# One decoder layer on one core: expert weights in units of 16 KB per partition, 11 ring slots for 22, and the last weights in plain order

## The chip, the core and the metric

One core of one Trainium2 chip runs the whole kernel. The metric is the device time of one execution in microseconds (us); lower is better. TensorE (PE) does the matrix products and, as a separate row, loads their stationary operands (PEld); VectorE (DVE) and ScalarE (ACT) do the elementwise work; SyncE (SP) issues nearly all DMAs.

## The reference

```python
# x: (256, 1024), one layer, fp32
a = hybrid_mixer(x)                        # x @ w_in (1024 x 3344), three groups of heads, @ w_out
x = layer_norm(ALPHA * x + a)
logits = x @ w_router + b_router           # 32 experts, 4 chosen for each token
gates  = softmax(top4(logits))
for e in chosen experts of a token:        # sum over its 4 experts, weighted by gates
    gu  = x @ w_gate_up[e] + b_gate_up[e]            # 1024 -> 2048
    g   = minimum(gu[:, ::2], 7); u = clip(gu[:, 1::2], -7, 7)
    act = (u + 1) * g * sigmoid(1.702 * g)
    m  += gate * (act @ w_down[e] + b_down[e])       # 1024 -> 1024
out = layer_norm(ALPHA * x + m + sigmoid(x @ w_ple_gate + b) * (p @ w_ple_proj))
```

The weights of one expert are 8 MiB (gate and up) and 4 MiB (down), fp32; the 32 experts are 384 MiB, and each is read once.

## The kernel before

**Work.** First the mixer: 13 column blocks of w_in (1 MiB each), each split into a high and a low fp32r part by ACT and DVE (`split`, L405) into one of three `whl` buffers, and multiplied by the split x; then the attention groups, w_out, the first norm and the router. Then a loop over the 32 experts (L1357). Tokens of an expert are gathered into 64 slots by one-hot matmuls (`gather`, L1015, for four experts at a time); an expert with more than 64 tokens takes a branch (`tc.If(n_of[e] > NSLOT)`) that does the rest in 32 further slots: `over_gather`, `over_up` (L1361, L1385) and, one iteration later, `over_scatter` and `over_down` (L1403). `expert_up` (L1090) makes gate and up: for each of eight k it reads one 1 MiB unit; PE shows 8 matrix instructions for a unit. `expert_evac` (L1104) copies the result out of PSUM with ACT and DVE; `expert_act` (L1109) transposes it on PE (tiles ptg, ptu) and runs `swiglu` (L1059: six DVE operations and one on ACT). `expert_down` (L1122) reads four 1 MiB units. In iteration e the order written is: first half of up(e), the sum of the pair before (`combine_pair`), second half of up(e), the branch of L1403 for e-1, down(e-1), evacuation and swiglu of e. The results of two experts are put together (`weigh`) and added to the output sum by `combine_pair`. Iterations 9 to 12 also do the per-layer embedding (`ple`).

**Weights.** SP moves everything into one ring of `RING = 22` slots of 8 KB per partition (1 MiB), named `u` in the profile. `want` (L183) puts loads into a list; `pump` (L190) issues the head of the list whenever a slot is free; `done(key)` (L200) frees a slot after its last reader. So the loads go out in the order of the list, which is the order of use, and the head waits until a slot is free. During the mixer the ring also holds its working buffers (`temp`, L205), during the experts `act`, `swi`, `acc` and `out`: activations, swiglu buffers and y, the output sum, and the weighed y. `swi` holds swiglu's g and sg, y, and also, in the same bytes as g and sg, what the branch of L1403 writes:

```python
        rm["g"], rm["sg"], rm["y"] = carve(loaded["swi"], (8, NSLOT), (8, NSLOT), (D,))
        rm["yo"], rm["CTo"], rm["Po"] = carve(loaded["swi"], (256,), (S,), (NT, 4 * NOVER))
```

**The end.** The list ends with gate and up 31, first half; down 30; gate and up 31, second half; down 31 (`w_last`, cut by columns 512, 256, 128, 128). `issue_after(mm.ins)` (L1417) holds the second half of up(31) behind down(30). Then `last_down` (tile pyl, L1453) and `last_combine` (pcbl) work by column blocks, and the second norm ends the kernel.

**Order on an engine.** The text's order is a wish: a planner in the framework places the instructions of each engine when the program is built, moves them where their data allow it, and adds the waits. A branch with its body stays one piece.

Of the kernel before, what the change touches and what calls it, by code (L numbers as in the profile page):

```python
# [21 lines left out]
P = 128  # L22
# [11 lines left out]
LEVELS = (256, 128, 64, 32, 16, 8, 4, 2)  # L34
RING = 22
NWARM = 30
# [6 lines left out]
NRUN = NE  # L43
# [70 lines left out]
def lay_out(inp):  # L114
# [14 lines left out]
    for g in range(4):  # L129
# [19 lines left out]
        "w_last": np.stack([*cols(w_last, 0, 512).reshape(P, 2, 2048).transpose(1, 0, 2), cols(w_last, 512, 256),  # L149
                            halves(w_last, 768)]),  # L150
        "b_down": a["b_down"],
# [7 lines left out]
def kernel(ctx, tc, x, xT_in, pT_in, w_in, w_out, diff_lambda, params, bgu_in, w_gate_up,  # L159
# [9 lines left out]

    free = list(range(RING))  # L170
    where = {}
    serial = [0]

    def slot_tile(dtype=F32, pick=0):
# [8 lines left out]
    def want(key, fn, dtype=F32):  # L183
        pending.append((key, fn, dtype))

    def aside(fn):

        pending.append((None, fn, None))

    def pump():  # L190
        while pending and (free or pending[0][0] is None):
            key, fn, dtype = pending.pop(0)
            if key is None:
                fn()
                continue
            t, s = slot_tile(dtype)
            where[key] = s
            loaded[key] = fn(t)

    def done(key):  # L200
        loaded.pop(key)
        free.append(where.pop(key))
        pump()

    def temp(key, dtype=F32, pick=-1):  # L205
        t, s = slot_tile(dtype, pick)
        where[key] = s
        loaded[key] = t
        return t

    def retake(old, key, dtype=F32):
        loaded.pop(old)
        free.append(where.pop(old))
        return temp(key, dtype)

# [55 lines left out]

    xT = temp("xT").rearrange("p (k t) -> p k t", k=NK)
    def load_first_cols(u):
# [18 lines left out]

    room = {3: "act", 5: "swi", 12: "acc", 24: "out"}
    n_want = RING
    for e in range(NRUN + 1):
        units = []
        if e < NRUN:
            units += [(("gu", e, k), load_flat(w_gate_up[0, e, k * P:(k + 1) * P, :])) for k in range(NK)]
        if e >= 1:
            for i in range(4):  # L300
                if e < NRUN:
                    fn = load_blocks(w_down[e - 1, i], 2)
                else:
                    fn = load_halves(w_last[i]) if i == 3 else load_blocks(w_last[i], 4 if i < 2 else NK)
                units.append((("dn", e - 1, i), fn))
        if e == NRUN - 1:
            units = units[:4] + units[8:] + units[4:8]
        if e == BIAS_AT:
            units.insert(0, ("bd", load_bd))
        if e == LN2_AT:  # L310
            units.append(("ln2", load_ln2))
        if e in PLE_AT:
            i = PLE_AT.index(e)
            if i == 0:
                units += [("x1T", lambda u: u), ("plt", lambda u: load_pT(u))]
            units.append((("ple", i), load_blocks(w_ple_gate[i], NK)))
        for key, fn in units:
            n_want -= 1
            if -n_want in room:
                key_ = room[-n_want]  # L320
                want(key_, lambda u: u, F32R if key_ == 'out' else F32)
            want(key, fn)
            if key[0] == "ple":
                aside(lambda i=key[1]: load_proj(i))
# [10 lines left out]

    xh = temp("xh", F32R).rearrange("p (k t) -> p k t", k=NK)
    xl = temp("xl", F32R).rearrange("p (k t) -> p k t", k=NK)
    whl = [temp(("w", i), F32R).rearrange("p (a n) -> p a n", a=2) for i in range(3)]
    ct = temp("ct")
    t1u, t2u, t3u, t4u, t5u, t6u, t7u = (temp(f"t{i}") for i in range(1, 8))  # L340
    A0, A1, qs, kk = carve(t1u, (4, S), (4, P), (S,), (S,))
# [63 lines left out]
    def split(half):  # L405

        w = whl[nsplit[0] % 3]
# [161 lines left out]
    def mixed(key, old, units):  # L569

        u = retake(old, key, F32R).rearrange("p (i a k t) -> p i a k t", i=2, a=2, k=2)
        for n, i in enumerate(units):
            mix[i] = u[:, n, 0], u[:, n, 1]
# [298 lines left out]
    for n, i in enumerate(WORDER):  # L872
# [14 lines left out]
        if n == 1:  # L887
            done("m0")
    for i in range(3):
        if i not in ((nsplit[0] - 1) % 3, (nsplit[0] - 2) % 3):  # L890
            done(("w", i))
# [22 lines left out]
    normalise(1, mv1)  # L914
    for i in range(3):
        if i in ((nsplit[0] - 1) % 3, (nsplit[0] - 2) % 3):
            done(("w", i))
# [172 lines left out]
    def expert_up(e, pgu=None, ks=range(NK)):  # L1090
# [31 lines left out]
    def expert_down(e, act, y):  # L1122
        py = ps_s("py")
        for f in range(8):
            blk, j = f // 2, f % 2
            w = loaded["dn", e, f // 2]
            for nb in range(2):
                mm = nc.tensor.matmul(py[nb * 64:(nb + 1) * 64, :], act[:, j * 4 + blk, :],  # L1128
                                      w[:, f % 2, nb * 512:(nb + 1) * 512], start=f == 0, stop=f == 7)
# [5 lines left out]
        return mm  # L1135

# [69 lines left out]
    def gu_part(e):  # L1206
        return lambda k, b: loaded["gu", e, k][:, b * 512:(b + 1) * 512]

    def dn_part(e):
        if e == NRUN - 1:  # L1210
            return lambda f, q: loaded["dn", e, q if q > 1 else f // 4][:, f if q > 1 else f % 4,
                                                                       *([] if q > 1 else [slice(q * 256, (q + 1) * 256)])]
        return lambda f, q: loaded["dn", e, f // 2][:, f % 2, q * 256:(q + 1) * 256]

# [13 lines left out]
    def general():  # L1228

        n_max = load_count(cnt[0:1, NE:NE + 1])  # L1230
        with tc.If(n_max > NSLOT + NOVER):
# [9 lines left out]
            with tc.For_i(0, NRUN, 1) as ie:  # L1241
# [3 lines left out]
                with tc.If(n > NSLOT + NOVER):  # L1245
                    with tc.For_i(0, (n - (NSLOT + 1)) // NOVER, 1):
                        def up(k, b):
                            w = wst[b % 2]
                            nc.gpsimd.dma_start(w, w_gate_up[0, bass.ds(ie, 1), k * P:(k + 1) * P,
                                                           b * 512:(b + 1) * 512].squeeze(0))  # L1250
                            return w

                        def down(f, q):
                            w = wst[q % 2][:, :256]
                            nc.gpsimd.dma_start(w, w_down[bass.ds(ie, 1), f // 2, :,
                                                        (f % 2) * 1024 + q * 256:(f % 2) * 1024 + (q + 1) * 256].squeeze(0))
                            return w
# [99 lines left out]
    for e in range(NRUN + 1):  # L1357
# [51 lines left out]
        if e >= 1:  # L1409
# [12 lines left out]
        if e == NRUN - 1:  # L1422
            tc.keep_in_program_order(nc.scalar.preload_act_table_set("natural_log_exp_and_others"))
        if e >= 1 and f % 2 == 1:
# [20 lines left out]
    def last_down(c0, n):  # L1445
        h = n // 2
        py = ps_z("pyl")
        for c in range(8):
            blk, j = c // 2, c % 2
            w = loaded["dn", f, c // 4 if n == 512 else c0 // 256]  # L1450
            w = w[:, c % 4] if n == 512 else w[:, c] if n == 256 else w[:, c, c0 % 256 // P]
            for hf in range(2):
# [50 lines left out]
```

## Time and profile before

| | |
|---|---|
| median of 3 runs | 1114.71 us (1114.48 to 1115.21) |
| the profiled execution | 1113.15 us, of it 1111.5 us from first to last instruction |
| PE busy | 1041.3 us (94%); PEld 519.0 us (47%) |
| DVE, ACT, GpSimd busy | 406.2, 194.6, 7.6 us |
| DMA | 433.65 MB, mean 390 GB/s |
| TensorE clock granted, mean | 0.983 of 2.4 GHz |

Stages in the profiled execution: mixer and router to about 151 us, experts from there, the last expert's down from 1087.85 us, the end at 1111.5 us. In the profile an L number is a line of the kernel; "x32" counts instructions; the bracket at the end of a line gives the idle time of that engine before it and what ended it. A stretch of PE rows in which each begins before the one above has ended is a PE without gaps.

### The profile page before, as it was taken

The page shows a single profiled execution, that of the slowest core. Times are in us where ns is not written, and L with a number is a line of the kernel's source. Part 1 is how long each engine was busy: PE and PEld are TensorE (multiplying, and loading weights), DVE is VectorE, ACT ScalarE, POOL GpSimd, SP SyncE. Part 2 cuts the span into 40 slices and gives each one's busy share as a digit, 9 for nine tenths or more (in the row PEclk, how much of TensorE's full clock was granted, in tenths as well). Part 3 has the DMA queues.
Part 4 walks back from the last instruction along what each step waited for, and adds up shares of the span by engine and source line. Part 5 has one row for each costly group of instructions (what it writes and reads, how often), then busy time and mean ns, then how long its engine had stood idle before and what let it go on. Part 6 is the DMA issues. An engine that isn't in the chain of part 4 may idle for free. (4 is left out here: it accounts for less than half of the span.)

```text
span 1111.5 us, 13836 instructions
## 1 busy us (share of the span) xinstructions
PE 1041.3 (94%) x5330; PEld 519.0 (47%) x5330; DVE 406.2 (37%) x865; ACT 194.6 (18%) x377; POOL 7.6 (1%) x19
## 2 busy tenths in 40 slices
PE   9999999999999999999999999979999999999995
PEld 7888854333433355554543334323433443334333
DVE  4977552333333323232333223313232223323235
ACT  4447541101110111100111111101110110101011
POOL 1000000000000000000000000000000000000000
PEclk9999999999999998999999999989999999999998
DMA  9956879999999999999999999999999999999981
GB/s 346 365 217 229 310 301 387 421 419 420 421 419 421 419 419 420 418 421 418 413 419 420 420 420 420 420 419 419 420 420 420 421 420 420 420 420 419 421 372 73
DMA packets 62414, 433.65 MB, mean 390 GB/s; under 512 B 6957, under 2 KB 7469, under 8 KB 10705
## 3 DMA queue, kind: packets, MB, share of 16 engines
q1 hardware_dynamic: 62114, 431.36, 94.5%
q8 instruction: 90, 1.47, 0.5%
q0 software_dynamic: 176, 0.53, 0.1%
q14 instruction: 34, 0.28, 0.1%
HBM read 430.81 MB, written 1.06 MB: 389 GB/s over the span
## 5 line engine op out<-in xcount | busy, mean ns | idle before, releaser
L1098 PE MATMUL pgu<-u,xe 128*64 128x512 f32 x2048 | 480.0, 596 | 6.9 <-PEq L1385 0.5
L1098 PEld LDWEIGHTS pgu<-u,xe 128*64 128x64 f32 x2048 | 162.2, 137 | 282.7 <-issue 272.2
L1128 PE MATMUL py<-u,u 128*64 128x512 f32 x992 | 227.6, 607 | 35.6 <-DVEq L1403 14.7
L1128 PEld LDWEIGHTS py<-u,u 128*64 128x64 f32 x992 | 83.4, 140 | 171.8 <-issue 123.8
L1107 DVE COPY u<-pgu 128x512 f32<-128x512 f32 x32 | 22.1, 692 | 207.2 <-PE pgu L1098 207.2
L1106 ACT COPY u<-pgu 128x512 f32<-128x512 f32 x32 | 18.7, 585 | 419.9 <-PE pgu L1098 419.9
L1062 DVE TENSOR_TENSOR u<-ptg,bgu 128x512 f32<-128x512 f32 x32 | 22.1, 690 | 182.5 <-PE ptg L1116 176.4
L1133 ACT COPY u<-py 64x512 f32<-64x512 f32 x31 | 17.9, 578 | 268.8 <-PE py L1128 268.8
L1088 DVE TENSOR_TENSOR u<-u,pcb 128x512 f32<-128x512 f32 x60 | 37.5, 683 | 52.9 <-PE pcb L1087 50.0
L412 DVE TENSOR_TENSOR u<-u,u 128x1024 fp32r<-128x1024 f32 x32 | 39.0, 1223 | 15.7 <-ACT u L411 14.2
L972 DVE TENSOR_SCALAR Pr<-ci,opos 128x32 fp32r<-128x32 f32 x64 | 13.5, 237 | 85.5 <-PEq L1361 83.5
L411 ACT CAST u<-u 128x1024 fp32r<-128x1024 f32 x32 | 33.4, 1048 | 27.0 <-PE pzt L423 9.7
L1293 PE MATMUL pleg<-u,u 128*128 128x256 f32 x128 | 32.2, 407 | 2.4 <-ACT u L979 2.1
L422 PE MATMUL pzt<-u,u 128*128 128x256 f32 x128 | 32.8, 291 | 0.3 <-ACT u L411 0.3
L1087 PE MATMUL pcb<-u,PT 128*128 128x512 f32 x120 | 32.5, 411 | 0.3
L423 PE MATMUL pzt<-u,u 128*128 128x256 f32 x128 | 32.3, 288 | 0.0
L1029 PE MATMUL pgx<-Pm,xnh 128*128 128x256 f32 (+1 forms) x128 | 31.0, 285 | 0.0
L1116 PEld LDWEIGHTS ptg<-ci,u 128*128 128x128 f32 x128 | 17.8, 207 | 26.5 <-issue 25.2
L1029 PE MATMUL pgx<-Pm,xnl 128*128 128x256 f32 (+1 forms) x128 | 30.2, 279 | 0.0
L1087 PEld LDWEIGHTS pcb<-u,PT 128*128 128x128 f32 x120 | 21.4, 189 | 17.3 <-issue 13.3
L1293 PEld LDWEIGHTS pleg<-u,u 128*128 128x128 f32 x128 | 25.7, 206 | 7.2 <-ACT u L979 2.3
L1029 PEld LDWEIGHTS pgx<-Pm,xnh 128*128 128x128 f32 x128 | 24.1, 188 | 6.5 <-issue 4.9
(289 smaller groups left out, 964.0 us busy)
## 6 DMA issues: line engine op xcount, KB each, us to landing
u<-in_w_gate_up_dram SPq DMA_DIRECT2D x256, 1024.0 KB, 18.3
u<-in_w_down_dram SPq DMA_DIRECT2D x124, 1024.0 KB, 19.8
u<-in_w_in_dram SPq DMA_DIRECT2D x11, 1024.0 KB, 16.6
u<-in_w_out_dram SPq DMA_DIRECT2D x4, 1024.0 KB, 7.5
u<-in_w_ple_gate_dram SPq DMA_DIRECT2D x4, 1024.0 KB, 17.8
u<-in_w_last_dram SPq DMA_DIRECT2D x3, 1024.0 KB, 19.7
u<-in_xT_dram SPq DMA_DIRECT2D x4, 256.0 KB, 5.8
u<-in_w_in_dram SPq DMA_DIRECT2D x4, 256.0 KB, 5.6
```

Source lines behind the costliest of these rows:

```text
L411: nc.scalar.copy(wh, half)
L412: nc.vector.tensor_tensor(wl, half, wh.bitcast(F32), op=ALU.subtract)
L422: nc.tensor.matmul(pz[:, j, :], wh[:, k, :], xh[:, k, :], start=k == 0, stop=False)
L423: nc.tensor.matmul(pz[:, j, :], wh[:, k, :], xl[:, k, :], start=False, stop=False)
L1029: nc.tensor.matmul(pg[:, j, :n], v[:, t, ch], hot, start=t + i == 0, stop=t + i == NT)
L1062: nc.vector.tensor_tensor(g, pg, bg, op=ALU.add)
L1087: nc.tensor.matmul(pcb, PT[:, t * P:(t + 1) * P], v[:, sl], start=i == 0, stop=i == 1)
L1088: nc.vector.tensor_tensor(yacc[:, t, sl], yacc[:, t, sl], pcb, op=ALU.add)
L1098: nc.tensor.matmul(pgu[b][hf * 64:(hf + 1) * 64, :], xe[:, k, c0:c0 + NSLOT], w[:, b * 1024 + hf * 512:b * 1024 + (hf + 1) * 512], start=k ...
L1107: nc.vector.tensor_copy(gs[:, 1, :], pgu[1])
L1128: mm = nc.tensor.matmul(py[nb * 64:(nb + 1) * 64, :], act[:, j * 4 + blk, :], w[:, f % 2, nb * 512:(nb + 1) * 512], start=f == 0, stop=f == 7)
L1293: nc.tensor.matmul(pg[:, j, :], w[:, k, sl], x1T[:, k, :], start=k == 0, stop=k == NK - 1)
```

## The change

The weights of gate and up, and of down, are laid out in DRAM so that 16 KB per partition are contiguous: two 1 MiB units become one 2 MiB DMA. The ring has 11 slots of 16 KB per partition. A slot can be given out in two halves of 8 KB, to two things of the same type; a load of one half takes a free half if there is one, and else opens a slot; a 2 MiB load needs a whole slot. The mixer's buffers share slots in pairs, `whl` has four buffers for three, and `m1` takes the place of `xl` for that of `t6`. `act` is asked for ahead of the first expert's weights. The loads of the last weights stand in plain order (gate and up 31, down 30, down 31), `issue_after` is gone, and in iteration 31 evacuation and swiglu of 31 are written ahead of the branch of L1403 and of down(30).

```diff
-RING = 22
+RING = 11
...
-        "w_gate_up": a["w_gate_up"], "w_down": np.stack([by_rows(w, 2) for w in a["w_down"][0]]),
+        "w_gate_up": np.stack([by_rows(w, 2) for w in a["w_gate_up"][0]]),
+        "w_down": np.stack([by_rows(w, 4) for w in a["w_down"][0]]),
...
-        t = ring.tile([P, 2048], dtype, name=f"u{serial[0]}", tag=f"slot{s}")
-        return t, s
+        t = ring.tile([P, 4096], dtype, name=f"u{serial[0]}", tag=f"slot{s}")
+        halves_of[s] = [t, dtype, {0, 1}]
+        return s
+
+    def take(key, s, which):
+        t, _, rest = halves_of[s]
+        rest.difference_update(which)
+        where[key] = s, which
+        return t[:, 2048 * min(which):2048 * (max(which) + 1)]
+
+    def half_of(dtype):
+        return next((s for s, (_, d, rest) in halves_of.items() if len(rest) == 1 and d == dtype), None)
+
+    def give(key):
+        s, which = where.pop(key)
+        rest = halves_of[s][2]
+        rest.update(which)
+        if len(rest) == 2:
+            halves_of.pop(s)
+            free.append(s)
...
     def pump():
-        while pending and (free or pending[0][0] is None):
-            key, fn, dtype = pending.pop(0)
+        while pending:
+            key, fn, dtype, size = pending[0]
+            s = half_of(dtype) if size == 1 else None
+            if key is not None and s is None and not free:
+                return
+            pending.pop(0)
...
+    want("act", lambda u: u)
+    room = {4: "swi", 12: "acc", 24: "out"}
...
-            units += [(("gu", e, k), load_flat(w_gate_up[0, e, k * P:(k + 1) * P, :])) for k in range(NK)]
-        if e >= 1:
...
-        if e == NRUN - 1:
-            units = units[:4] + units[8:] + units[4:8]
+            units += [(("gu", e, j), load_flat(w_gate_up[e, j]), 2) for j in range(4)]
+        if 1 <= e < NRUN:
+            units += [(("dn", e - 1, j), load_blocks(w_down[e - 1, j], 4), 2) for j in range(2)]
+        if e == NRUN:
+            units += [(("dn", e - 1, 0), load_blocks(w_last[:, :4096], 8), 2),
+                      (("dn", e - 1, 2), load_blocks(w_last[:, 4096:6144], 8), 1),
+                      (("dn", e - 1, 3), load_halves(w_last[:, 6144:]), 1)]
...
-    whl = [temp(("w", i), F32R).rearrange("p (a n) -> p a n", a=2) for i in range(3)]
+    whl = [u.rearrange("p (a n) -> p a n", a=2) for n in (0, 2) for u in temps(("w", n), ("w", n + 1), dtype=F32R)]
+    t1u, t2u = temps("t1", "t2")
+    t3u, t5u = temps("t3", "t5")
+    t4u, t6u = temps("t4", "t6")
+    ct, t7u = temps("ct", "t7")
...
-    done("xl")
...
-    mixed("m1", "t6", (1, 2))
+    mixed("m1", "xl", (1, 2))
+    done("t6")
...
         for k in ks:
-            w = loaded["gu", e, k]
+            w = loaded["gu", e, k // 2][:, k % 2 * 2048:(k % 2 + 1) * 2048]
...
-            done(("gu", e, k))
+            if k % 2:
+                done(("gu", e, k // 2))
...
-            w = loaded["dn", e, f // 2]
+            w = loaded["dn", e, f // 4]
...
-            if f % 2:
-                done(("dn", e, f // 2))
+            if f % 4 == 3:
+                done(("dn", e, f // 4))
...
-        if e < NRUN - 1:
+        if e < NRUN:
             expert_up(e, gs_of[e], range(2 if e == 1 else NK // 2, NK))
+        if e == NRUN - 1:
+            expert_evac(gs_of.pop(e))
+            act_of[e] = expert_act(e)
+            tc.keep_in_program_order(nc.scalar.preload_act_table_set("natural_log_exp_and_others"))
...
-            mm = expert_down(f, act_of.pop(f), y)
-        if e == NRUN - 1:
-            with tc.issue_after(mm.ins):
-                expert_up(e, gs_of[e], range(NK // 2, NK))
-        if 0 < e < NRUN:
+            expert_down(f, act_of.pop(f), y)
+        if 0 < e < NRUN - 1:
             expert_evac(gs_of.pop(e))
             act_of[e] = expert_act(e)
```

## Rows read from the trace of the kernel before

**Rows 1.** The page: DMA busy share in tenths, 40 slices of the span.
```profile
DMA  9956879999999999999999999999999999999981
```

**Rows 2.** Windows: length, busy us of each engine (instructions), clock, DMA share, GB/s.
```profile
200.00:1060.00 860.00, 812.70 (x3786) 354.32 (x3784) 260.43 (x515) 100.01 (x176) 0.00 (x0) 0.98 1.01 420
...
0.00:150.00 150.00, 145.59 (x1067) 125.47 (x1068) 105.79 (x269) 80.92 (x175) 5.79 (x18) 1.00 0.78 298
```

**Rows 3.** Waits of PE from 200 to 1075 us: total, times, longest.
```profile
PE py L1128 <- DVEq L1403: 14.7, 16, 1.3
...
PE py L1128 <- DMA u<-in_w_last_dram: 1.6, 1, 1.6
...
PE py L1128 <- DMA u<-in_w_gate_up_dram: 0.9, 1, 0.9
```

**Rows 4.** The last load of down 23, by tile, 847 to 849 us.
```profile
L239 SPq DMA_DIRECT2D u<-in_w_down_dram x1: 328/328/328, 848.1 to 848.1; - x1
...
DMA to landing us min/median/max: 19.8/19.8/19.8
```

**Rows 5.** PE's timeline, start and length: down 23.
```profile
863.97 7.09 PE L1128 MATMUL py<-u,u 128*64 128x512 f32 x32 [0.89 <-DVEq L1403]
```

**Rows 6.** DMA packets and queue, 10.8 to 13.8 and 600 to 700 us.
```profile
DMA packets 517, 1.26 MB, mean 420 GB/s; under 512 B 60, under 2 KB 234, under 8 KB 505
...
q1 hardware_dynamic: 517, 1.26, 105.5%
...
DMA packets 5758, 42.02 MB, mean 420 GB/s; under 512 B 638, under 2 KB 638, under 8 KB 638
...
q1 hardware_dynamic: 5746, 41.85, 100.7%
```

**Rows 7.** Issue to landing of gate-and-up loads, 500 to 545 and 770 to 1045.
```profile
DMA to landing us min/median/max: 9.7/12.3/16.6
...
DMA to landing us min/median/max: 19.5/19.8/20.9
```

**Rows 8.** SP's timeline, 30 to 170 us: the first experts' loads.
```profile
60.00 69.92 SPq L252 DMA_DIRECT2D u<-in_w_gate_up_dram  x16
```

**Rows 9.** PE's timeline at the first expert.
```profile
151.31 6.23 PE L1098 MATMUL pgu<-u,xe 128*64 128x512 f32 x28 [0.30 <-PEq L1361]
```

**Rows 10.** Waits of PE from 14 to 150 us, the mixer: first and last of four.
```profile
PE pzn L440 <- DVE u L412: 0.8, 1, 0.8
...
PE pzt L422 <- ACT u L411: 0.3, 1, 0.3
```

**Rows 11.** PE's timeline, the end: start, length, idle before.
```profile
1065.19 2.14 PE L1087 MATMUL pcb<-u,PT 128*128 128x512 f32 x8
1068.91 7.09 PE L1128 MATMUL py<-u,u 128*64 128x512 f32 x32 [1.58 <-DMA u<-in_w_last_dram]
1075.80 7.07 PE L1098 MATMUL pgu<-u,xe 128*64 128x512 f32 x32
...
1084.11 0.52 PE L1116 MATMUL ptu<-ci,u 128*128 128x128 f32 x3
1087.85 7.11 PE L1453 MATMUL pyl<-u,u 128*64 128x256 f32 x64 [3.22 <-DVEq L1403]
```

**Rows 12.** DVE's timeline, the end: last swiglu operation of expert 31.
```profile
1087.11 0.69 DVE L1068 TENSOR_TENSOR u<-u,u 128x512 f32<-128x512 f32 x1
```

**Rows 13.** Windows ahead of, in and behind the start of pyl.
```profile
1082.90:1087.80 4.90, 1.39 (x8) 1.00 (x8) 4.04 (x7) 1.75 (x2) 0.00 (x0) 1.00 0.52 212
1088.00:1091.30 3.30, 3.30 (x18) 1.79 (x18) 0.00 (x0) 0.00 (x0) 0.00 (x0) 0.50 0.09 31
```

**Rows 14.** SP's timeline: the first three loads of down 31.
```profile
1062.31 5.29 SPq L239 DMA_DIRECT2D u<-in_w_last_dram  x3
```

**Rows 15.** All engines' timeline, 964.5 to 968.5: an ordinary expert.
```profile
966.63 0.69 DVE L1107 COPY u<-pgu 128x512 f32<-128x512 f32 x1 [7.12 <-PE pgu L1098]
...
967.48 1.51 PE L1128 MATMUL py<-u,u 128*64 128x512 f32 x6 [0.89 <-DVEq L1403]
```

More of the change, by code (lines that the diff above doesn't have):

```diff
@@ L147, in lay_out @@
         "diff_lambda": a["diff_lambda"], "params": r, "bgu": bgu.reshape(P, 512),
-        "w_gate_up": a["w_gate_up"], "w_down": np.stack([by_rows(w, 2) for w in a["w_down"][0]]),
-        "w_last": np.stack([*cols(w_last, 0, 512).reshape(P, 2, 2048).transpose(1, 0, 2), cols(w_last, 512, 256),
-                            halves(w_last, 768)]),
+        "w_gate_up": np.stack([by_rows(w, 2) for w in a["w_gate_up"][0]]),
+        "w_down": np.stack([by_rows(w, 4) for w in a["w_down"][0]]),
+        "w_last": np.concatenate([cols(w_last, 0, 512), cols(w_last, 512, 256), halves(w_last, 768)], axis=1),
         "b_down": a["b_down"],
@@ L195, in pump, with temps, retake @@
                 continue
-            t, s = slot_tile(dtype)
-            where[key] = s
-            loaded[key] = fn(t)
+            if s is None:
+                s = open_slot(dtype)
+            loaded[key] = fn(take(key, s, (0, 1) if size == 2 else (min(halves_of[s][2]),)))
     def done(key):
         loaded.pop(key)
-        free.append(where.pop(key))
+        give(key)
         pump()
[L205 to L214, printed above, removed]
+    def temps(*keys, dtype=F32):
+        s = open_slot(dtype, -1)
+        for n, key in enumerate(keys):
+            loaded[key] = take(key, s, (n,))
+        return [loaded[key] for key in keys]
+    def retake(old, key):
+        loaded[key] = loaded.pop(old)
+        where[key] = where.pop(old)
+        return loaded[key]
     def carve(t, *shapes):
@@ L270 @@
     mp = mixer.enter_context(tc.tile_pool(name="mp", bufs=1))
-    xT = temp("xT").rearrange("p (k t) -> p k t", k=NK)
+    xT = temps("xT")[0].rearrange("p (k t) -> p k t", k=NK)
     def load_first_cols(u):
@@ L291 @@
     aside(lambda: load_third())
-    room = {3: "act", 5: "swi", 12: "acc", 24: "out"}
-    n_want = RING
+    want("act", lambda u: u)
+    room = {4: "swi", 12: "acc", 24: "out"}
+    n_want = 2 * RING - 2
     for e in range(NRUN + 1):
@@ L297 @@
         if e < NRUN:
-            units += [(("gu", e, k), load_flat(w_gate_up[0, e, k * P:(k + 1) * P, :])) for k in range(NK)]
-        if e >= 1:
[L300 to L305, printed above, removed]
-        if e == NRUN - 1:
-            units = units[:4] + units[8:] + units[4:8]
+            units += [(("gu", e, j), load_flat(w_gate_up[e, j]), 2) for j in range(4)]
[5 more added lines that the diff above has]
+                      (("dn", e - 1, 3), load_halves(w_last[:, 6144:]), 1)]
         if e == BIAS_AT:
-            units.insert(0, ("bd", load_bd))
+            units.insert(0, ("bd", load_bd, 1))
         if e == LN2_AT:
-            units.append(("ln2", load_ln2))
+            units.append(("ln2", load_ln2, 1))
         if e in PLE_AT:
@@ L314 @@
             if i == 0:
[L315 to L322, printed above, removed]
+                units += [("x1T", lambda u: u, 1), ("plt", lambda u: load_pT(u), 1)]
+            units.append((("ple", i), load_blocks(w_ple_gate[i], NK), 1))
+        for key, fn, size in units:
+            n_want -= size
+            for at in [a for a in room if a <= -n_want]:
+                key_ = room.pop(at)
+                want(key_, lambda u: u, *((F32R, 2) if key_ == "out" else (F32, 1)))
+            want(key, fn, F32, size)
             if key[0] == "ple":
@@ L334 @@
     nc.vector.memset(onec, 1.0)
-    xh = temp("xh", F32R).rearrange("p (k t) -> p k t", k=NK)
-    xl = temp("xl", F32R).rearrange("p (k t) -> p k t", k=NK)
-    whl = [temp(("w", i), F32R).rearrange("p (a n) -> p a n", a=2) for i in range(3)]
-    ct = temp("ct")
-    t1u, t2u, t3u, t4u, t5u, t6u, t7u = (temp(f"t{i}") for i in range(1, 8))
+    xh, xl = (u.rearrange("p (k t) -> p k t", k=NK) for u in temps("xh", "xl", dtype=F32R))
+    whl = [u.rearrange("p (a n) -> p a n", a=2) for n in (0, 2) for u in temps(("w", n), ("w", n + 1), dtype=F32R)]
[3 more added lines that the diff above has]
+    ct, t7u = temps("ct", "t7")
     A0, A1, qs, kk = carve(t1u, (4, S), (4, P), (S,), (S,))
@@ L405, in split @@
     def split(half):
-        w = whl[nsplit[0] % 3]
+        w = whl[nsplit[0] % 4]
         nsplit[0] += 1
@@ L569, in mixed @@
     def mixed(key, old, units):
-        u = retake(old, key, F32R).rearrange("p (i a k t) -> p i a k t", i=2, a=2, k=2)
+        u = retake(old, key).rearrange("p (i a k t) -> p i a k t", i=2, a=2, k=2)
         for n, i in enumerate(units):
@@ L888 @@
             done("m0")
-    for i in range(3):
-        if i not in ((nsplit[0] - 1) % 3, (nsplit[0] - 2) % 3):
+    for i in range(4):
+        if i not in ((nsplit[0] - 1) % 4, (nsplit[0] - 2) % 4):
             done(("w", i))
@@ L914 @@
     normalise(1, mv1)
-    for i in range(3):
-        if i in ((nsplit[0] - 1) % 3, (nsplit[0] - 2) % 3):
+    for i in range(4):
+        if i in ((nsplit[0] - 1) % 4, (nsplit[0] - 2) % 4):
             done(("w", i))
@@ L1125, in expert_down @@
             blk, j = f // 2, f % 2
-            w = loaded["dn", e, f // 2]
+            w = loaded["dn", e, f // 4]
             for nb in range(2):
-                mm = nc.tensor.matmul(py[nb * 64:(nb + 1) * 64, :], act[:, j * 4 + blk, :],
-                                      w[:, f % 2, nb * 512:(nb + 1) * 512], start=f == 0, stop=f == 7)
-            if f % 2:
-                done(("dn", e, f // 2))
+                nc.tensor.matmul(py[nb * 64:(nb + 1) * 64, :], act[:, j * 4 + blk, :],
+                                 w[:, f % 4, nb * 512:(nb + 1) * 512], start=f == 0, stop=f == 7)
+            if f % 4 == 3:
+                done(("dn", e, f // 4))
         r = (e % 2) * 64
@@ L1206, in gu_part @@
     def gu_part(e):
-        return lambda k, b: loaded["gu", e, k][:, b * 512:(b + 1) * 512]
+        return lambda k, b: loaded["gu", e, k // 2][:, k % 2 * 2048 + b * 512:k % 2 * 2048 + (b + 1) * 512]
     def dn_part(e):
         if e == NRUN - 1:
-            return lambda f, q: loaded["dn", e, q if q > 1 else f // 4][:, f if q > 1 else f % 4,
-                                                                       *([] if q > 1 else [slice(q * 256, (q + 1) * 256)])]
-        return lambda f, q: loaded["dn", e, f // 2][:, f % 2, q * 256:(q + 1) * 256]
+            return lambda f, q: (loaded["dn", e, q][:, f] if q > 1 else
+                                 loaded["dn", e, 0][:, f, q * 256:(q + 1) * 256])
+        return lambda f, q: loaded["dn", e, f // 4][:, f % 4, q * 256:(q + 1) * 256]
     def over_pos(e):
@@ L1449, in last_down @@
             blk, j = c // 2, c % 2
-            w = loaded["dn", f, c // 4 if n == 512 else c0 // 256]
-            w = w[:, c % 4] if n == 512 else w[:, c] if n == 256 else w[:, c, c0 % 256 // P]
+            w = loaded["dn", f, c0 // 256][:, c]
+            w = w[:, c0 % 256 // P] if n == P else w
             for hf in range(2):
```

20 lines of the change are left out of this document (9 added, 11 removed).

## The prediction

> **What bounds the kernel now.** The first thing to look at is the DMA strip [rows 1]: from the eighth slice on every digit is a 9, and the window over the expert stage gives a DMA share of 1.01 at 420 GB/s [rows 2]. Taken alone, this says that the weights' stream sets the time. The same window has PE busy for 812.7 of 860 us, so the shares do not decide it. A wait decides it: if the stream set the time, PE would again and again stand idle until a load lands. PE's waits in the expert stage name a DMA twice, 1.6 and 0.9 us, and what else is named is the branch of L1403 [rows 3]; the 1.6 us names weights that the instruction behind the wait does not read, and I count it as the branch too.
>
> The next question is by how much the stream is ahead, and this can be worked out for any load from its issue, its time to landing and its first reader. The narrowest place that I found is down 23: its fourth and last unit goes out at 848.1 us and needs 19.8 us, so it lands at 867.9 us [rows 4]; PE starts down 23 at 863.97 us and runs through in 7.09 us [rows 5], so the fourth quarter is wanted at 863.97 + 0.75 x 7.09 = 869.3 us. That is 1.4 us to spare with both resources full. So PE bounds the expert stage and the stream follows close behind. A faster stream alone gives nothing; one that falls back by more than 1.4 us costs what lies beyond. The mixer is PE's too: 145.6 of 150 us busy [rows 2].
>
> **The 2 MiB loads.** How much faster they move is bounded from two stretches with different packets [rows 6]. Between 10.8 and 13.8 us, 517 packets less 60 small ones, 457, carry 1.26 MB, 2757 bytes each, and take 1.055 x 16 engines x 3.0 us = 50.6 us, 110.8 ns each. Between 600 and 700 us, 5758 less 638, 5120 packets of 8 KB, take 1.007 x 16 x 100 = 1611 us, 314.7 ns each. A line through both has 0.0375 ns a byte and 7.4 ns a packet. A row of 16 KB as one packet would take 622 ns where two take 629: 1.2% less. The other end is zero, if a row still goes as two packets. I take 1.2%, since the line fits both stretches; the time of the kernel gets 0 from it, because PE is the bound.
>
> The Trainium skill, "DMA: Bandwidth & Descriptors", section Bandwidth, measures 425 GB/s for 16 MB against 341 GB/s for 1 MB in one transfer and so speaks for larger loads. By its 425 GB/s the stream would gain as much as by the line (425 against the trace's 420 is also 1.2%).
>
> **The shallower ring.** Before, act, swi, acc, out leave 18 of 22 MiB for weights, 17 once ln2 is in. After, act, swi, acc and ln2 are halves of two slots and out is one: 8 slots, 16 MiB. In experts 9 to 12, x1T, plt and ple hold two more slots wholly or by half: 12 to 14 MiB where there were 15 or 16. What the missing 2 to 4 MiB are worth is read from the time to landing [rows 7]. From 770 us on it is 19.8 us at the median and never under 19.5, eight loads of 2.5 us in flight; there a smaller ring still keeps several 2 MiB loads in flight. From 500 to 545 us it is 9.7 to 16.6 us, four to six in flight, and with 2 to 4 fewer the stream can run dry. Bounds for what it loses there: 0, and two 2 MiB loads (9.9 us). Against the upper one speaks that PE is slow there because of the embedding and frees slots late in both kernels; I take 2 us. From 545 to 868 us the faster packets win back 323 x 1.2% = 3.9 us. At down 23 the stream is then 1.9 us earlier. But its third and fourth units now land together, wanted when the third begins, 863.97 + 0.5 x 7.09 = 867.5 us, against 867.9 - 1.9 = 866.0: 1.5 us to spare, no stall. Without the faster packets it would be 867.9 + 2 - 867.5 = 2.4 us of stall.
>
> **The mixer.** With slots in pairs, the first load of expert 0 needs a slot that is wholly free, so it goes out later than at the 60 us of before (when t1 and t2 are both done), the last of expert 1 when the w_out splits are through. The first reader starts at 151.3 us [rows 8, 9]: hidden; there are 91 us of cover from the old issue on. The fourth `whl` buffer can remove waits for a split, and m1's new place a wait for gog and rgg; PE's waits in this stretch are 0.8, 0.7, 0.5 and 0.3 us [rows 10]. So it is worth between 0 and -2.3 us, or a little worse if the planner orders it differently (I bound that by the same 2.3). I take 0. Half as many issues on SP (328 ns each [rows 4]) are nothing: SP issues ahead, and PE does not wait for it.
>
> **The end.** Here the change touches the path. Before [rows 11, 12, 13]: combine_pair ends at 1067.33; 1.58 us at the branch; down(30) 7.09; the second half of up(31) 7.07 to 1082.87; then the evacuation, the transposes (1082.79 to 1084.63) and swiglu, whose last operation ends at 1087.80; pyl starts at 1087.85. PE does 1.39 us of work in these 4.9 us, and when pyl starts, the granted clock is 0.50, the 1.2 GHz level, for some 3.3 us. That is 1.7 us of pyl's 7.11 lost.
>
> After, the second half of up(31) comes first, then evacuation and swiglu, then down(30). Swiglu's 4.9 us from evacuation to the last operation then run beside down(30)'s 7.09 on PE, with 2 us of cover. Sum from 1067.33: 7.07 + 1.84 + 7.09 + 1.58 for the branch = 17.6, pyl at 1084.9 instead of 1087.85: -2.9 us. If PE stays occupied, the fall of the clock is avoided too: between 0 and -1.7 us; I take -1.0, since one short wait remains. The last loads are in time: down 31 now goes out behind down 30, its first two units went out at about 1062.3 and 1065 us before [rows 14] and need some 20 us, so 1085 us, less the 1.9 us gained at 868 and a further 200 x 1.2% = 2.4.
>
> Sum: 0 (stream) + 0 (mixer) - 2.9 - 1.0 = -3.9 us. The profiled execution took 1113.15 us, 1.65 more than its span and 1.56 under the median of the runs; the difference is applied to the median: 1114.71 - 3.9 = 1110.8 us.
>
> **Rivals.**
> *PE stands behind the branch.* The branch of L1403 writes yo, CTo and Po into the bytes of g and sg, so for expert 30 it must now follow swiglu(31). down(30) stands behind it in the text, and PE has waited for DVE at just this place, 0.89 us [rows 15]. If it stays there, PE idles through swiglu: 1067.33 + 7.07 + 4.9 + 0.89 + 7.09 + 1.58 = 1088.9, which is 1.1 us later than before: 1115.8 us. Against it: the evacuation at L1107, which the text puts behind down, runs ahead of it [rows 15], so the planner does move work across this branch, and down(30) needs nothing of it.
>
> *The stream comes late.* This is the case on the slower side. Place: down 23 at 864 to 868 us. If the stretch from 430 to 545 us costs the stream two 2 MiB loads, 9.9 us, of which 3.9 come back, it is 6.0 + 0.4 = 6.4 us late: 1110.8 + 6.4 = 1117.2 us. Each us beyond the 1.5 to spare counts; over 6.1 us of stall the kernel is slower than before by more than can be told from no change.
>
> *The stream is the bound after all.* Then 1.2% of 860 us come off: 1114.7 - 10.3 = 1104.4 us. For it speaks the share of 1.01; against it the 1.4 us to spare even at the narrowest place. The Trainium skill, "Perfetto Trace Analysis", section Identifying the Most-Contended Engine, calls the matmul row's busy share a poor measure and wants the weight loads' share; here that is 354 of 860 us [rows 2], and by this rule the DMA would be the most contended and this case right. The landing times disagree.
>
> **How the numbers follow.** Overlap at the end and no stall 0.52 (1107.8 to 1113.5), behind the branch 0.25 (1113.5 to 1117.5), stream late 0.15 (1113 to 1120), stream as the bound 0.08 (1103 to 1107). The predicted time is that of the first; the range that leaves out no more than two in ten is 1106 to 1117.5. 0.2% is 2.2 us, about what a measurement of this kernel can tell from no change. Faster: 0.46 of the first and the last, 0.54; the same: 0.06 + 0.19 + 0.05 = 0.30; slower: 0.06 + 0.10 = 0.16.
>
> **What would show it.** The loads of gate and up: half as many, of 2 MiB, and a window over 600 to 700 us at about 425 GB/s (420: no faster packets). PE's waits of the expert stage still name hardly a DMA, and the last load of down 23 lands ahead of PE's reading of it. At the end, pyl starts 3 us sooner behind combine_pair, swiglu(31) lies beside py on PE, and the window behind pyl's start has the clock at 1.00. A stretch of py or pgu that ends on a DMA, at expert 23 or in 430 to 560 us, would make it wrong upwards; an idle PE beside swiglu(31) would show the first rival; a new order in the mixer that moves the first expert by more than 2 us would be outside the sum.

## The result

The changed kernel takes 1108.49 us at the median of four runs (1107.60 to 1109.14), the kernel before 1114.96 us beside it: ratio 0.994, interval 0.9927 to 0.9953. Run once more in a later comparison it took 1108.97 against 1114.28 us, ratio 0.997, interval 0.9951 to 0.999. So it is 0.3 to 0.6% faster. Of the ten later runs four took 1112.64 to 1114.59 us, at a mean granted clock of 0.979 or 0.980 where the others had 0.983 to 0.985; and one run of before_odd, told below, took 1823.55 us at a clock of 0.554 and is left out of its median and ratio. The profiled execution took 1109.14 us with a span of 1107.4 us, 4.1 us less than the span before.

The page of the changed kernel, DMA share and rate in 40 slices of 27.7 us, against [rows 1]:

```profile
DMA  9835699999999999999999999999999999999991
GB/s 346 325 151 178 274 377 428 426 426 428 426 425 427 426 423 415 425 424 394 403 428 426 426 426 426 427 425 426 426 427 424 428 427 425 427 427 427 424 383 61
```

DMA packets and queue of the changed kernel from 600 to 700 us, which answer to [rows 6]:

```profile
DMA packets 2921, 42.60 MB, mean 426 GB/s; under 512 B 320, under 2 KB 320, under 8 KB 320
## 3 DMA queue, kind: packets, MB, share of 16 engines
q1 hardware_dynamic: 2910, 42.44, 100.0%
```

A row of 16 KB does go as one packet (42.6 MB in 2921 packets, of which 320 are small: 16.4 KB in each of the 2601 others), and the stream runs at 426 GB/s where it had 420. From 166 us to the last two slices it is full, except in the two slices from 498 to 554 us (394 and 403 GB/s) and, by less, in the one from 415 to 443 us (415 GB/s).

PE's waits from 200 to 1075 us at the branch of over_down (L1430, before L1403) and for weights, to be set beside [rows 3]:

```profile
PE py L1152 <- DVEq L1430: 13.3, 15, 0.9
...
PE py L1152 <- DMA u<-in_w_down_dram: 2.5, 2, 1.3
...
PE pgu L1121 <- DMA u<-in_w_gate_up_dram: 1.0, 1, 1.0
```

PE's timeline at the end (start, length, idle before it), against [rows 11]; first the changed kernel, then two lines of the kernel before:

```profile
1053.64 7.09 PE L1121 MATMUL pgu<-u,xe 128*64 128x512 f32 x32
...
1071.44 0.52 PE L1140 MATMUL ptu<-ci,u 128*128 128x128 f32 x3
1075.28 9.68 PE L1152 MATMUL py<-u,u 128*64 128x512 f32 x32 [3.31 <-DVEq L1430]
1084.77 3.19 PE L1475 MATMUL pyl<-u,u 128*64 128x256 f32 x26
...
1095.97 1.49 PE L1484 MATMUL pcbl<-u,CT 128*128 128x128 f32 x8
```

```profile
1058.17 7.09 PE L1098 MATMUL pgu<-u,xe 128*64 128x512 f32 x32
...
1100.03 1.49 PE L1462 MATMUL pcbl<-u,CT 128*128 128x128 f32 x8
```

Three windows of the changed kernel, with the columns of [rows 13]:

```profile
1072.00:1075.20 3.20, 0.00 (x0) 0.00 (x0) 2.98 (x6) 1.82 (x2) 0.00 (x0) 0.77 0.79 329
1075.30:1080.50 5.20, 5.20 (x14) 1.70 (x16) 0.00 (x0) 0.00 (x0) 0.00 (x0) 0.50 0.56 231
1080.50:1084.70 4.20, 4.20 (x22) 1.55 (x20) 0.00 (x0) 0.00 (x0) 0.00 (x0) 0.99 0.23 94
```

The end is not what was forecast: PE stands for 3.31 us at the branch of over_down (L1430) while VectorE runs swiglu of expert 31, and its clock is at 0.50, the 1.2 GHz level, for the next 5.2 us. From the first matmul of up(31) to the end of the last pcbl the changed kernel takes 1095.97 + 1.49 - 1053.64 = 43.82 us. Before, it is 1100.03 + 1.49 - 1058.17 = 43.35 us. So the end lost 0.5 us, and the whole gain was there when expert 31 began, 4.53 us earlier than before.

**Where it comes from.** The first expert begins at 151.30 us as before [rows 9], and by the starts of up and down PE gains in two kinds of steps. Three large ones (0.85 us between experts 9 and 10, 1.69 us in expert 16, 1.59 us between 29 and 30) lie where the clock of the kernel before was at 0.50 for longer than that of the changed kernel; 0.65 us are lost between 19 and 20, where it was the other way round. Such stretches differ between executions of one kernel: at 872 to 879 us the changed kernel's was 3.4 us long here and 6.8 us in after_again.

The others are steps of 0.80 or 0.81 us, at experts 4, 6, 8, 18, 26 and 28 (PE loses steps of 0.84 and 0.82 us at 22 and 23). What differs there is the order of PE's instructions. An up has 32 matmuls, and they come in pairs: hf = 0 and hf = 1 write the two 64-row halves of one PSUM tile. The second branch over over_up (L1408, before L1385) stands somewhere in the second half of up, where the planner put it. Behind an odd number of matmuls it cuts a pair. In the program before, 25 experts have a cut pair (22 by this branch, 3 by that of over_down), in the changed one 20: at 4, 6, 8, 18, 24, 26 and 28 the branch stood behind 17 or 27 matmuls and now stands behind 24, where the last 2 MiB unit begins.

What a cut pair costs is seen in the second half of up, PE's timeline: in the changed kernel expert 27 (cut) and expert 28 (whole), then expert 28 of the kernel before (cut). A matmul here counts as two:

```profile
956.20 3.65 PE L1121 MATMUL pgu<-u,xe 128*64 128x512 f32 x14
959.99 4.48 PE L1121 MATMUL pgu<-u,xe 128*64 128x512 f32 x18 [0.15 <-PEq L1408]
...
981.14 3.65 PE L1121 MATMUL pgu<-u,xe 128*64 128x512 f32 x16
984.95 3.65 PE L1121 MATMUL pgu<-u,xe 128*64 128x512 f32 x16 [0.16 <-PEq L1408]
```

```profile
983.26 5.36 PE L1098 MATMUL pgu<-u,xe 128*64 128x512 f32 x22
988.78 2.76 PE L1098 MATMUL pgu<-u,xe 128*64 128x512 f32 x10
```

Seven matmuls take the 3.65 us of eight, and the nine behind the branch 4.48 us: from its start to its end the cut half takes 8.27 us, the whole one 7.46 us, 0.81 us less, and the same half of the kernel before 8.28 us. The two matmuls of a pair run side by side; where the branch cuts a pair, one matmul on either side of it is left alone and takes the time of a pair. Five cut pairs fewer are 4.05 us. Up to expert 31 the clock was at 0.50 for 20.5 us in place of 27.3, worth up to 3.4 us. The waits for loads took part of this back, all at one place, the second half of up 24 and down 23:

```profile
856.31 3.65 PE L1121 MATMUL pgu<-u,xe 128*64 128x512 f32 x16 [0.97 <-DMA u<-in_w_gate_up_dram]
861.31 3.65 PE L1152 MATMUL py<-u,u 128*64 128x512 f32 x16 [1.34 <-DMA u<-in_w_down_dram]
866.09 3.65 PE L1152 MATMUL py<-u,u 128*64 128x512 f32 x16 [1.12 <-DMA u<-in_w_down_dram]
```

They are 3.4 us; the first two stand where the branches cost PE 0.16 and 0.89 us elsewhere, so 2.4 us are new. The sum, 4.05 + 3.4 - 2.4 = 5.0 us, is near the 4.53 us read. In these two executions the clock is nearly as large a term as the pairs; what belongs to the change, the runs below decide.

### The profile page after: what moved, and what is told of

Same layout as the page of the kernel before. It is cut to its first block, busy times and chain, and to the rows that moved or that the text cites. A ratio compares the mean times of both kernels' runs of the same rounds, so it can differ in the third digit from the quotient of the medians.

```text
span 1107.4 us, 13426 instructions
## 1 busy us (share of the span) xinstructions
PE 1034.3 (93%) x5330; PEld 513.7 (46%) x5330; DVE 405.8 (37%) x865; ACT 194.8 (18%) x377; POOL 7.6 (1%) x19
## 5 line engine op out<-in xcount | busy, mean ns | idle before, releaser
L1121 PEld LDWEIGHTS pgu<-u,xe 128*64 128x64 f32 x2048 | 159.6, 137 | 282.2 <-issue 277.8
L1087 ACT ACTIVATE u<-u 128x512 f32<-128x512 f32 x32 | 19.9, 623 | 40.7 <-DVE u L1086 40.6
```

## The experiments

Three theories were open, with the letters of the expectations: PE is the only bound and its cut pairs made the gain (B), the faster stream made it (C), or it takes both, because PE and the stream are two bounds that lie close together (A). The experiments put the branch where it was wanted.

**The branch fixed.** `expert_up` writes the branch itself, behind `at` matmuls of the second half; for the experts from 2 on nothing else changes but that a unit is given back only behind the branch, which reads it too:

```diff
-    def expert_up(e, pgu=None, ks=range(NK)):
+    def expert_up(e, pgu=None, ks=range(NK), at=0, branch=None):
...
+                    with tc.issue_after(behind) if behind else nullcontext():
+                        mm = nc.tensor.matmul(pgu[b][hf * 64:(hf + 1) * 64, :], xe[:, k, c0:c0 + NSLOT], ...)
+                    n += 1
+                    if n == at:
+                        with tc.issue_after(mm.ins):
+                            branch()
+                        behind = nc.cur_bb.bb.instructions[-1]
...
+            expert_up(e, gs_of[e], range(2 if e == 1 else NK // 2, NK), 8 if e > 1 else 0, over)
+        if e == BIAS_AT:
+            output_bias()
```

With 8 the branch stands between whole pairs, behind 24 of 32 ("even"), with 7 inside one ("odd"). The output bias of expert 3 had to go behind the branch, since its tile shares a buffer with what the branch reads.

Of after_even was expected:

> The changed kernel with the branch in the second half of up fixed between whole pairs (24 of an expert's 32 pgu matmuls ahead of it) for experts 2 to 31. In the changed kernel it stands inside a pair for 18 experts, and a pair that is cut costs about 0.81 us (four matmuls one after the other, 0.43 us each, where whole pairs run two at a time). Theory A (PE and the stream of weights are both bounds, close together): PE has about 15 us less work, but the stream ran full at 426 to 428 GB/s from 166 us on except for about 4 us at 498 to 554 us, so no more than 2 to 5 us comes out: 1104 to 1107 us, and PE now waits for loads. Theory B (PE alone is the bound): 1093 to 1095 us. Theory C (the branch's place costs nothing, the gain came from the faster stream alone): 1108 to 1109 us.

Of after_odd was expected:

> The same, but with the branch fixed inside a pair (23 of 32 matmuls ahead of it) for all 30 experts, 11 or 12 cut pairs more than the changed kernel has. Theories A and B: PE is the bound here, 9 us more (11 times 0.81): 1116 to 1119 us. Theory C: 1108 to 1109 us.

Of before_even was expected:

> The kernel before (loads of 8 KB rows, 22 slots) with its branch fixed between whole pairs for experts 2 to 30; it has 22 cut pairs there. Theory A: its stream was full at 418 to 421 GB/s from 195 us to the end, so that 18 us less work on PE gives at most 0 to 2 us: 1113 to 1115 us, and PE waits for loads from expert 23 on. Theory B: 1095 to 1098 us. Theory C: 1114 to 1115 us, for another reason, and PE's time in the second half of up does not change.

Of before_odd was expected:

> The kernel before with the branch fixed inside a pair for experts 2 to 30, 7 cut pairs more than it has. Theories A and B: 5 to 6 us more, 1119 to 1121 us. Theory C: 1114 to 1115 us.

| run | loads | cut pairs | median us | ratio to before, interval |
|---|---|---|---|---|
| before | 1 MiB | 25 | 1114.52 | |
| before_even | 1 MiB | 0 | 1114.26 | 0.9998 (0.9988 to 1.0007) |
| before_odd | 1 MiB | all 29 of 2 to 30 | 1124.56 | 1.0077 (1.0052 to 1.0101) |
| after_even | 2 MiB | 1 | 1104.75 | 0.9913 (0.9897 to 0.993) |
| after_odd | 2 MiB | all 30 of 2 to 31, and one more | 1119.86 | 1.0052 (1.0035 to 1.0069) |

Theory A holds: without any cut pair the kernel before is no faster at all, and the changed one gains nearly 4 us more, where B wanted 1093 to 1095 us of it and C no change. Where the time that PE saves in before_even goes is seen in PE's timeline, down 21 of before and of before_even, then down 23 of before_even (before: [rows 5]):

```profile
813.20 3.23 PE L1128 MATMUL py<-u,u 128*64 128x512 f32 x14 [0.90 <-DVEq L1403]
```

```profile
803.59 5.73 PE L1139 MATMUL py<-u,u 128*64 128x512 f32 x24 [0.89 <-DVEq L1417]
809.87 1.94 PE L1139 MATMUL py<-u,u 128*64 128x512 f32 x8 [0.54 <-DMA u<-in_w_down_dram]
...
863.89 1.94 PE L1139 MATMUL py<-u,u 128*64 128x512 f32 x8 [0.90 <-DVEq L1417]
866.05 1.94 PE L1139 MATMUL py<-u,u 128*64 128x512 f32 x8 [0.23 <-DMA u<-in_w_down_dram]
868.50 1.94 PE L1139 MATMUL py<-u,u 128*64 128x512 f32 x8 [0.51 <-DMA u<-in_w_down_dram]
870.97 1.94 PE L1139 MATMUL py<-u,u 128*64 128x512 f32 x8 [0.54 <-DMA u<-in_w_down_dram]
```

PE is 9.6 us ahead at down 21 and level with before at down 23, where it waits for unit after unit. In after_even the same happens at 426 GB/s: it is 8.2 us ahead of the changed kernel at down 21 and 2.7 at down 23.

after_odd is 0.9 us and before_odd some 4 us over what was expected, though before_odd has only four cut pairs more than before (29 against 25, where the expectation counted seven), some 3.2 us. Most of the rest is the clock: up to PE's last work it was at 0.50 for 44 us of before_odd's profiled execution, in the kernel before for 31. Of the 44 us 3.4 lie at expert 3, behind the output bias that now follows the branch. PE's timeline of after_even there, where down takes 8.79 us for 7.09 (8.74 in after_odd, 8.78 in before_odd):

```profile
238.15 3.69 PE L1356 MATMUL pbd<-u,GT 32*128 32x512 f32 x8 [0.78 <-DVE GT L1351]
242.73 8.79 PE L1163 MATMUL py<-u,u 128*64 128x512 f32 x32 [0.89 <-DVEq L1444]
```

PE's waits in after_even, 200 to 1075 us (the changed kernel's: 2.5 and 1.0):

```profile
PE py L1163 <- DMA u<-in_w_down_dram: 5.4, 4, 1.6
PE pgu L1123 <- DMA u<-in_w_gate_up_dram: 5.1, 6, 1.2
```

**The size of a load alone, with whole pairs.** after_even, with each 2 MiB load of the expert weights (but w_last) issued as two of 1 MiB from the layout of the kernel before:

```diff
-            units += [(("gu", e, j), load_flat(w_gate_up[e, j]), 2) for j in range(4)]
+            units += [(("gu", e, j), load_two(*(w_gate_up[0, e, k * P:(k + 1) * P, :] for k in (2 * j, 2 * j + 1))), 2) for j in range(4)]
```

Of after_even_8k was expected:

> The changed kernel with the branch between whole pairs, ring of 11 slots of 16 KB as it is, but each expert load of 2 MiB issued as two of 1 MiB with rows of 8 KB (the layout of the kernel before in memory). PE's order is the same, so only the stream changes. Theory A: the stream is the bound, 420 in place of 427 GB/s, and by expert 23 (863 us, from 194 us on) it comes 9 to 11 us later than with rows of 16 KB: 1113 to 1116 us, about the time of the kernel before with whole pairs, 1114.3 us. If the size of a row does nothing for the time and whole pairs do it all: 1104 to 1106 us.

1114.90 us, ratio 0.9995 (0.9984 to 1.0006): the 10 us that after_even gained are all gone. The stream is back at 420 GB/s, and PE's waits from 200 to 1075 us name loads for 16 us:

```profile
PE pgu L1130 <- DMA u<-in_w_gate_up_dram: 6.7, 15, 0.6
PE py L1170 <- DMA u<-in_w_down_dram: 6.6, 12, 1.2
...
PE py L1170 <- DMA u<-in_w_gate_up_dram: 2.7, 3, 0.9
```

**The size of a load alone, with the cut pairs of before.** The changed kernel, and for each expert the place of the branch as in the kernel before:

```diff
+CUT = (0, 0, 0, 0, 1, 7, 11, 7, 11, 7, 0, 5, 3, 1, 5, 7, 5, 5, 11, 7, 0, 0, 2, 2, 11, 7, 11, 7, 11, 7, 5, 0)
...
+            expert_up(e, gs_of[e], range(2 if e == 1 else NK // 2, NK), CUT[e], over)
```

after_cut_as_before, with the output bias behind the branch, and after_cut_as_before2, with the output bias in its old place:

Of after_cut_as_before was expected:

> The changed kernel with the branch of up put, expert by expert, where it stands in the kernel before (25 cut pairs in place of 20), all else as changed. It tells how much of the gain is the stream's alone. If five cut pairs more cost 0.8 to 1.0 us each on a PE that is the bound here: 4 to 5 us more than the changed kernel, 1112 to 1114 us, so that the larger loads alone gave some 2 us. If the stream gave the gain: 1108 to 1109.5 us.

Of after_cut_as_before2 was expected:

> As the run that put the branch of up where it stands in the kernel before, but with the four matmuls of the output bias in expert 3 left ahead of up's second half, where both kernels have them; in that run they had moved behind the branch, and PE lost 3.6 us between expert 2's down and expert 4. 25 cut pairs, as in the kernel before. If PE is the bound with these cut pairs and the larger loads do nothing by themselves, PE goes through the experts at the pace of the kernel before: 1113 to 1115.5 us. If the larger loads gave part of the gain by themselves: 1110 to 1112 us; all of it: 1108 to 1109.5 us.

Of after_again was expected:

> The changed kernel unchanged, beside the two others: 1108 to 1109.5 us.

The first gave 1117.90 us, ratio 1.003 (1.0013 to 1.0048), 4 us over the expectation; its PE lost 3.6 us on the changed kernel up to expert 4, where the bias had moved and the clock was at 0.50 for 6.8 us. The second gave 1115.65 us, ratio 1.0001 (0.999 to 1.0012); after_again, 1108.97 us, is told above. The profiled execution of the second, its slowest, is 5.5 us behind before at expert 4 (1.7 from the mixer; for 6.8 us at expert 3 the clock was at 0.50), and stays 4 to 5.5 us behind up to expert 25: with the same pairs cut, PE goes at the pace of before, whatever the loads. So the larger loads, with the smaller ring and the new end, give no gain that shows by themselves, as fewer cut pairs by themselves give none.

**The end alone, in the kernel before.**

```diff
-        if e == NRUN - 1:
-            units = units[:4] + units[8:] + units[4:8]
...
-        if e < NRUN - 1:
+        if e < NRUN:
             expert_up(e, gs_of[e], range(2 if e == 1 else NK // 2, NK))
+        if e == NRUN - 1:
+            expert_evac(gs_of.pop(e))
+            act_of[e] = expert_act(e)
```

Of before_plain was expected:

> The kernel before with the end alone in plain order: expert 31's second half of up, its transposes and its swiglu ahead of the branch of over_down and of down 30, and the loads in that order; 22 slots of 8 KB rows as before. The prediction's step for the end gave 2.9 us less, 3.9 with the clock: 1111 to 1112 us. Its rival that PE stands behind the branch until swiglu has ended gave 1.1 us more, the trace of the changed kernel 1.5 us more; with one more cut pair at expert 31 (0.8 us) 1116 to 1118 us.

1115.12 us, ratio 0.9995 (0.9983 to 1.0007): neither 3 us less nor 1 us more. The wait is there. PE's timeline of before_plain:

```profile
1059.14 7.09 PE L1096 MATMUL pgu<-u,xe 128*64 128x512 f32 x32
...
1081.59 8.79 PE L1126 MATMUL py<-u,u 128*64 128x512 f32 x32 [3.31 <-DVEq L1405]
...
1101.37 1.49 PE L1459 MATMUL pcbl<-u,CT 128*128 128x128 f32 x8
```

From up(31) to the end it takes 43.72 us against 43.35. The plain order trades idle times of 1.58 and 3.22 us [rows 11] and a fall of the clock in pyl for one idle time of 3.31 us, a fall in py (8.79 in place of 7.09 us) and one more cut pair, at expert 31. The last branch also moves into pyl, behind 26 of its 64 rows, and cuts a pair there. Up to expert 30 the branches over over_up stand where they stood in the kernel before: the new end alone does not move them.

**down 30 ahead of the branch.**

```diff
+        if e == NRUN - 1:
+            y = rm["y"]
+            expert_down(e - 1, act_of.pop(e - 1), y, False)
         if e >= 1:
             pos, acto = ov_of.pop(e - 1)
             with tc.If(n_of.pop(e - 1) > NSLOT):
```

(`False` leaves its weights held until the branch, which reads them, is through.)

Of after_overlap was expected:

> The changed kernel with down 30 written ahead of the last but one branch of over_down, behind the transposes of expert 31; nothing else moved. In the changed kernel PE stood 3.3 us at that branch while VectorE ran swiglu, and its clock fell right behind. If the wait is the branch's, the 7.1 us of down 30 now cover swiglu, and the last down starts at 1080 to 1081 us in place of 1084.8 (its first load lands at 1079.5): 3 to 5 us less, 1104 to 1105.5 us. If something else ends last there (a load, the output's way), the wait moves and the time stays within 1 us of 1108.5 us.

Of after_even_overlap was expected:

> Both: the branch of up fixed between whole pairs, and down 30 ahead of the branch of over_down. The two gains lie in different places (experts 3 to 31 and the end): 1104.75 us less 3 to 4 us, 1100.5 to 1102 us; the first load of the last down, which landed at 1076.8 us in the run with whole pairs, is what ends last then. If the end was already held by the stream, no more than 1 us comes out: 1103.5 to 1105 us.

after_overlap 1105.08 us, ratio 0.9906 (0.9881 to 0.9932); with whole pairs, after_even_overlap, 1102.29 us, ratio 0.989 (0.9862 to 0.9917), the fastest of all and faster than both kernels. PE's timelines of the two, at the end:

```profile
1072.35 7.09 PE L1152 MATMUL py<-u,u 128*64 128x512 f32 x32
1079.74 6.00 PE L1482 MATMUL pyl<-u,u 128*64 128x256 f32 x84 [0.31 <-PEq L1433]
```

```profile
1071.63 3.65 PE L1163 MATMUL py<-u,u 128*64 128x512 f32 x16 [0.76 <-DMA u<-in_w_down_dram]
1076.58 6.00 PE L1496 MATMUL pyl<-u,u 128*64 128x256 f32 x84 [1.30 <-DMA u<-in_w_last_dram]
```

swiglu is covered, no clock falls there, and pyl starts at 1079.74 in place of 1084.77 us. With whole pairs the last loads are what PE waits for: the stream holds the end too.

**Every down ahead of its branch.** The same lines, with `1 <= e < NRUN` as the condition, on after_even:

Of after_even_ahead was expected:

> Whole pairs, and each expert's down ahead of the branch of over_down, not only down 30: that takes the waits behind this branch (23 us in all between 200 and 1050 us in the run with whole pairs) off PE in every expert. If the stream is the bound with whole pairs, it gives nothing over the run with down 30 alone ahead (1102.3 us): 1101 to 1104 us, with more waits for loads. If PE were still the bound: 1085 to 1090 us.

1126.66 us, ratio 1.0127 (1.0105 to 1.0149), a miss on the wrong side, and no test of the stream. The transposes that follow now stand behind the branch, and the branch behind VectorE's work on y. PE's waits, 200 to 1050 us:

```profile
PE ptg L1151 <- DVEq L1449: 35.2, 20, 2.4
```

Behind up the branch costs 0.89 us, for then VectorE has only the copy of pgu to do; behind a down, up to 2.4 us. The clock fell to 0.50 14 times as well, against 7 in after_even_overlap. A place that is good at the end is bad in the loop.

## Why the prediction was right, and where it was not

The time lies in the range and the sign is as forecast, but by luck: the case that the forecast is the sum of, swiglu covered at the end, did not come about, and the gain came from a term that the sum does not have.

**The bound.** PE bounds the kernel before, and the stream follows closely: both shown. At equal cut pairs larger loads change nothing (1.0001), and down 23, where 1.4 us were to spare, is where before_even has fallen back to the pace of before. Taking PE's work as fixed was the gap: the prediction read PE as a bound with a given length, and never looked at how the branch lies in it. Its reading that all other waits name the branch of L1403 is too short, since DVE's opos (8.9 us) and the branch at L1231 (7.2 us) are named as well; none of these is a load, so the conclusion stands.

**The 2 MiB loads.** 426 against 420 GB/s is 1.4%, forecast 1.2%. "The time of the kernel gets 0 from it" holds for the loads alone; but they moved the second bound by some 10 us (after_even against after_even_8k), and without that not even 25 cut pairs fewer gain anything (before_even). What the Trainium skill, "DMA: Bandwidth & Descriptors", section Bandwidth, measured, 425 GB/s for 16 MB against 341 GB/s for 1 MB, agrees with the trace in its direction; its 341 GB/s is not what a stream of 1 MiB loads moved here, 420.

**The ring.** It did run dry where forecast. The slices from 498 to 554 us have 394 and 403 GB/s, 27.7 x (33 + 24) / 427 = 3.7 us lost against 2. The second unit of down 23 was forecast to land at 866.0 us, and PE's wait for it ended at 866.09. That no stall follows was wrong by little, since PE came there 2.7 us earlier than before: 3.4 us of waits, 1.1 us in after_again. The smaller ring itself costs next to nothing: with whole pairs and rows of 8 KB, 11 slots gave a ratio of 0.9995 (after_even_8k), 22 slots 0.9998 (before_even).

**The mixer.** 0, as forecast: expert 0 begins at 151.30 us against 151.31.

**The end.** This is the step of the sum that failed: "Swiglu's 4.9 us ... then run beside down(30)'s 7.09 on PE", 3.9 us with the clock. The first rival's mechanism took place, PE behind the branch; the planner did not move down 30 across it. The rival's price, 1.1 us more, was also too high: 0.4 to 0.5 us by the traces, nothing by the time of before_plain. after_overlap shows that the gain was there to be had: pyl starts 5.0 us earlier than in the changed kernel, and the time is 3.4 us less.

**The rival that the stream is the bound** had 0.08. For the kernel before it is wrong by the 1.4 us to spare, and for the same kernel with whole pairs right. It drew on the Trainium skill, "Perfetto Trace Analysis", section Identifying the Most-Contended Engine, which does not judge PE by the matmul row but wants the weight loads' share among others. Taken so, the DMA would have been the bound and 1104.4 us the forecast; the waits of PE decided better. The figure is about what the stream allowed once PE's pairs were whole: after_even took 1104.75 us.

**What no part of the text had:** that the change moves the places where the planner puts the branches. What in it does so was not isolated; the new end does not (before_plain), so the units of 2 MiB and their ring are left. That the new places are at 24 because the last unit begins there is argued from the order alone. The sum of 3.9 us met the 4.0 us between the two profiled executions by chance.

## What to carry to other kernels

- A planner that places the instructions itself can move a branch in work that the change does not touch. Compare the order of the instructions on the bounding engine, before any term is costed; and fix by hand what must not be cut: a branch between paired matmuls, not inside.
- Two bounds that lie this close hide each other. Either change alone measured nothing here (0.9998 and 1.0001), both together 0.9% (after_even). "No effect" of one change is no reason to drop it; try the pair.
- A branch that several engines take is a meeting place: here what stood behind it on PE waited for VectorE's work ahead of it. Long work of PE that needs nothing of the branch goes ahead of it only where PE would stand idle behind it.

## What the runs showed of the hardware

- Two matmuls on tiles of 64 columns each (128*64 in the rows) ran side by side; one alone took as long as a pair, 0.81 us more for each pair cut by a branch.
- Weights in rows of 16 KB came at 426 GB/s, in rows of 8 KB at 420, the latter in the rings of 22 and of 11 slots.
- After PE had stood for 3.3 us the clock was at 0.50, for some 5 us of py in the changed kernel and for some 3.4 us in before_plain (an estimate: its py took 1.70 us more than 7.09); with the idle time gone, in after_overlap, py took 7.09 us where it had taken 9.68. In after_cut_as_before2 it fell at expert 3 with no long idle time ahead, behind the matmuls on 32 rows of the output bias; why there and not in the changed kernel stays open.
